# Two chained transformer blocks on one core: token blocks of the split activations 132 columns apart, and rows of scales, queries, attention visits and norm inputs moved

## The chip, the cores and the metric

The kernel runs on one core of a Trainium2 chip (trn2). The metric is the device time of one execution in microseconds (us).

## The reference

256 tokens of width 1024 go through two blocks of two layers each. Every layer is a mixer and a feed-forward part, each behind a norm and added to the stream x. The mixers are, in order: attention with forget gates (fox), attention with a compressed key and value (MLA), gated linear attention in chunks of 64 tokens (GLA), and a short convolution. Cut to what matters:

```
for layer in range(2):                                   # first block
    h = rms_norm(x, norm_mix_g[layer])
    x = x + (fox_mixer(h, ...) if layer == 0 else mla_mixer(h, ...))
    x = x + sq_relu_mlp(rms_norm(x, norm_ffn_g[layer]), w_up, w_down)
x = rms_norm(x, final_norm_g)
for i in range(2):                                       # second block
    h = rmsnorm(x, norm_mix_g_2[i])
    x = x + (gla_mixer(h, ...) if i == 0 else short_conv_mixer(h, ...))
    x = x + conv_ffn(rmsnorm(x, norm_ffn_g_2[i]), w_up, conv_w, w_down)
return rmsnorm(x, final_norm_g_2)
```

In the fox mixer the logits are `q @ k * scale + cum(query) - cum(key)`, where `cum` is a running sum of log sigmoids; in GLA the keys and queries are multiplied by exponentials of such sums, and the scores of a chunk are masked.

## The kernel before

All weights come from memory in float32. Each matrix product is made of three: a value is split into a high part (a cast to the matmul's own 32-bit format) and a low part (what is left), and a product is `hh*wh + hh*wl + hl*wh`. ACT casts the weights (L294), DVE subtracts for their low part (L312). The activations' parts hh and hl lie in tiles of the class Act, [128, 4, 256]: 128 rows of the width, four such blocks k, 256 tokens (L92). The token halves t=0 and t=1 of one k lie 128 columns, 512 bytes, apart.

Three shapes of products fill most of the time. `proj_T` (L391) makes a transposed result: 128 weight columns are loaded as the stationary operand, and the 256 tokens of hh or hl move past. `proj` and `accum` make rows of tokens: 128 tokens of hh or hl are stationary, and 512 weight columns move. `proj_wide` (L421) does the same with 264 columns. All go through `mmw` (L341), which lets the moving operand run alternately through its two halves; the distance within a pair is 512 bytes in `proj_T`, 1024 in `proj` and `accum`, 528 in `proj_wide`.

The order of the work is set in two steps. The program calls `tick()` after each group of 3 matmuls of 512 columns or 6 of 256. A step that has to come later is put into a queue with `after(n, fn)` and is emitted n ticks later; the distances stand in the list DLY. The visits of the two attentions come from a generator that is asked every so many ticks, by the tables FOX and MLA: each entry has a number of ticks and the heads whose weighted sum, transposes and logits are then emitted. A tile scheduler then puts each engine's instructions into their order.

The places that the change touches:

- `make_row` (L137) copies two columns of per-token scales on DVE to full width (L144), transposes them on PE (L523) and copies the result on ACT into a row "rowb". Rows scale transposed results (`by_row`, L419).
- `norm` (L588): an x tile that a projection has finished is transposed DLY[1] ticks later (`prep`, L523) and multiplied by the gain on DVE (L546); DLY[0] ticks later it is split (`split`, L509 on ACT, L512 on DVE). In `final_norm` (L1106), at the end of the first block, every x tile is also multiplied by a gain row (L1122), and, once POOL has the statistics of all four, by a scale (L1136). This ends at the entry of GLA, whose first product is a `proj_wide`.
- `split_pair` (L1368) and `split_ctx` (L729) split hidden values (L1373 on ACT, L1374 on DVE) and attention results.
- `fox` (L820): log sigmoids and their running sums (`cumulate`, DLY[6]), then visits by FOX. `mla` (L993): visits by MLA. In a visit, probabilities p (L697, L707, L716) are transposed (L533), copied to pT (L725), and used for the weighted sum (`pT,v` on L339).
- `gla` (L1151): `proj_T` of keys into PSUM tiles named acc, `proj_T` of queries into tiles named up, both scaled from PSUM on DVE (L419) and multiplied into kT (L1232) and qT (L1240). Then `core` (L1261) makes masked scores in up tiles, while the next projections also use up tiles.

`mmw` in full:

```
def mmw(self, out, lhsT, rhs, start, stop):
    self.mm(out.rearrange("p (b a) -> p b a", a=2), lhsT, rhs.rearrange("p (a b) -> p b a", a=2), start, stop)
```

## Time and profile before

| | us |
|---|---|
| median of 3 runs | 1104.34 |
| the runs | 1104.15, 1104.34, 2274.76 |
| the profiled execution | 1104.49 |
| its span in the trace | 1102.7 |

The span runs from the first to the last instruction of the trace; the profiled execution's own time is 1.8 us more. TensorE's granted clock was 0.997 of full speed, the upper of its two levels, so times of matmuls can be compared between stages. In the trace, PE is a matmul, PEld a weight load, which overlaps the matmul before it; DVE, ACT and POOL are the vector, scalar and GpSimd engines. A form is a group of like instructions with their shapes. In the trace's names, hh, hl, wh and wl are the parts of activations and weights, up, acc and tp PSUM tiles, and "out<-in" lists the operands of an instruction; with matmuls the first of the two inputs is the one that moves.

### The profile page before, as it was taken

How to read it: one execution, taken by the hardware profiler on the slowest of the kernel's cores; microseconds unless marked ns; L12 is line 12 of the kernel's file. 1: busy time of each engine (PE TensorE's matmuls, PEld its weight loads, DVE VectorE, ACT ScalarE, POOL GpSimd, SP SyncE). 2: the span in 40 equal slices, each digit the busy share in tenths (PEclk: the TensorE clock that was granted, in tenths of full speed). 3: DMA queues.
4: the chain of work that ended last, by engine and by line, in shares of the span. 5: the costliest groups of instructions: out<-in, count | busy, mean ns of one | idle time of the engine just before them, and what ended most of it. 6: DMA issues, size and time to landing. Idle time of an engine off the chain costs nothing.

```text
span 1102.7 us, 19201 instructions
## 1 busy us (share of the span) xinstructions
PE 1087.3 (99%) x7769; PEld 1003.4 (91%) x7769; DVE 801.4 (73%) x1200; ACT 609.2 (55%) x927; POOL 30.4 (3%) x55
## 2 busy tenths in 40 slices
PE   9999999999999999999999999999999999999997
PEld 7987999999988999999897899999999999999996
DVE  6687756556687766555788578787787768987786
ACT  6466655445665555545664556555555446565563
POOL 1000000000000000000010000000000000000001
PEclk9999999999999999999999999999999999999998
DMA  9844466655563566665555354566665664657551
GB/s 335 298 165 145 162 195 206 210 193 173 142 207 128 172 192 204 206 200 192 194 180 183 108 178 155 179 197 217 201 220 193 197 204 153 189 194 224 188 166 74
DMA packets 137801, 207.30 MB, mean 188 GB/s; under 512 B 10528, under 2 KB 65008, under 8 KB 137712
## 3 DMA queue, kind: packets, MB, share of 16 engines
q1 hardware_dynamic: 136576, 203.89, 56.8%
q10 hardware_dynamic: 1136, 2.17, 0.5%
q8 instruction: 61, 1.00, 0.4%
q14 instruction: 28, 0.23, 0.1%
HBM read 204.97 MB, written 1.07 MB: 187 GB/s over the span
## 4 chain that ended last, share of the span: by engine, by line
PE 87%; DVE 7%; ACT 2%; DMA 1%; issue 1%; SPq 0%; ACTq 0%; DVEq 0%
PE up L339 52%; PE acc L339 33%; DVE wl L312 2%; DMA raw<-fox_w_in 1%; ACT wh L294 1%; PE acc L523 1%; PE tp L523 1%; ACT p L697 1%; DVE p L716 1%; DVE x L602 0%; DVE p L707 0%; PE tp L533 0%; DVE tmp L1365 0%; DVE pT L725 0%; DVE kT L1232 0%
## 5 line engine op out<-in xcount | busy, mean ns | idle before, releaser
L312 DVE TENSOR_TENSOR wl<-raw,wh 128x1024 fp32r<-128x1024 f32 (+2 forms) x373 | 452.3, 1219 | 223.4 <-ACT wh L294 222.4
L294 ACT CAST wh<-raw 128x1024 fp32r<-128x1024 f32 (+2 forms) x373 | 388.8, 1043 | 381.7 <-PE up L339 253.1
L339 PE MATMUL up<-hh,wh 128*128 128x256 f32 x1564 | 431.7, 276 | 0.0
L339 PE MATMUL up<-hh,wl 128*128 128x256 f32 x1564 | 430.1, 275 | 0.0
L339 PE MATMUL up<-hl,wh 128*128 128x256 f32 x1564 | 429.4, 275 | 0.0
L339 PEld LDWEIGHTS up<-hh,wh 128*128 128x128 f32 x1564 | 300.1, 192 | 2.9 <-issue 1.5
L339 PEld LDWEIGHTS up<-hh,wl 128*128 128x128 f32 x1564 | 300.1, 192 | 0.9
L339 PEld LDWEIGHTS up<-hl,wh 128*128 128x128 f32 x1564 | 299.8, 192 | 0.3 <-DVE hl L512 0.2
L339 PE MATMUL acc<-wh,hh 128*128 128x512 f32 (+1 forms) x606 | 227.4, 375 | 0.2 <-DVE mx L716 0.2
L339 PE MATMUL acc<-wh,hl 128*128 128x512 f32 (+1 forms) x606 | 225.1, 371 | 0.1
L339 PE MATMUL acc<-wl,hh 128*128 128x512 f32 (+1 forms) x606 | 224.8, 371 | 0.0
L339 PEld LDWEIGHTS acc<-wh,hl 128*128 128x128 f32 x606 | 114.5, 189 | 15.4 <-DVE hl L1374 0.5
L339 PEld LDWEIGHTS acc<-wh,hh 128*128 128x128 f32 x606 | 114.6, 189 | 15.0 <-DVE mx L716 0.6
L339 PEld LDWEIGHTS acc<-wl,hh 128*128 128x128 f32 x606 | 114.7, 189 | 13.4
L1365 DVE SCALAR_TENSOR_TENSOR tmp<-tmp,vecs,tmp 128x255 f32<-128x255 f32 x192 | 78.0, 479 | 15.2 <-ACT tmp L1363 15.2
L339 PE MATMUL up<-wh,hh 128*128 128x512 f32 (+4 forms) x142 | 52.2, 370 | 1.8 <-DVE tmp L419 1.8
L339 PE MATMUL up<-wl,hh 128*128 128x512 f32 (+4 forms) x142 | 49.9, 352 | 0.2 <-DVE wl L312 0.2
L339 PE MATMUL up<-wh,hl 128*128 128x512 f32 (+4 forms) x142 | 49.8, 353 | 0.1
L1363 ACT ACTIVATE tmp<-tmp,vecs 128x256 f32<-128x256 f32 x96 | 40.9, 496 | 0.0
L1373 ACT CAST hh<-tmp 128x512 fp32r<-128x512 f32 x58 | 34.1, 619 | 8.3 <-DVE tmp L1418 8.3
L1374 DVE TENSOR_TENSOR hl<-tmp,hh 128x512 fp32r<-128x512 f32 x58 | 38.3, 685 | 0.0
L339 PEld LDWEIGHTS up<-wh,hh 128*128 128x128 f32 x142 | 26.8, 189 | 8.1 <-issue 5.5
(205 smaller groups left out, 769.8 us busy)
## 6 DMA issues: line engine op xcount, KB each, us to landing
raw<-ffn_w_up SPq DMA_DIRECT2D x176, 256.0 KB, 4.2
raw<-ffn_w_up SPq DMA_DIRECT2D x32, 1024.0 KB, 5.3
raw<-ffn_w_down SPq DMA_DIRECT2D x32, 1024.0 KB, 5.0
raw<-ffn_w_down SPq DMA_DIRECT2D x44, 512.0 KB, 6.6
raw<-sc_w_in SPq DMA_DIRECT2D x12, 1024.0 KB, 5.3
raw<-fox_w_in SPq DMA_DIRECT2D x10, 1024.0 KB, 9.7
raw<-gla_w_in SPq DMA_DIRECT2D x10, 1024.0 KB, 5.0
raw<-fox_w_out SPq DMA_DIRECT2D x4, 1024.0 KB, 5.2
```

Of the source, the lines that this page charges most:

```text
L294: self.last_hi = nc.scalar.copy(hi[:, :kn, :w], self.raws[r][:, k:k + kn])
L312: self.last_wl = nc.vector.tensor_tensor(out=u.lo[:, :kn, :w], in0=self.raws[r][:, k:k + kn], in1=u.hi[:, :kn, :w].bitcast(F32), op=ALU.su ...
L339: self.nc.tensor.matmul(out, lhsT, rhs, start=start, stop=stop, skip_group_check=True)
L523: self.nc.tensor.transpose(tp[:, i * P:(i + 1) * P], src[:, i * P:(i + 1) * P], self.ident)
L697: self.nc.scalar.activation(out=p[:, o:o + n], in_=p[:, o:o + n], func=AF.Exp, scale=scale, bias=nm[:, j:j + 1], accum_out=sm[:, j:j + 1])
L716: self.nc.vector.tensor_tensor_reduce(out=p[:, o:o + n], in0=lgs[h][:, w], in1=bias(h)[:, w], scale=1.0, scalar=NEG, op0=ALU.add, op1=ALU. ...
L1363: nc.scalar.activation(out=out, in_=z, func=AF.Copy, scale=w[:, 2:3])
L1365: nc.vector.scalar_tensor_tensor(out=out[:, d:], in0=z[:, :S - d], scalar=w[:, 2 - d:3 - d], in1=out[:, d:], op0=ALU.mult, op1=ALU.add)
L1373: nc.scalar.copy(hi, src)
L1374: nc.vector.tensor_tensor(out=lo, in0=src, in1=hi.bitcast(F32), op=ALU.subtract)
```

## The change

Six edits are made together.

1. The tiles of hh and hl become [128, 4, 2, 132], of which 128 columns are used: the two token halves lie 528 bytes apart. `block`, `get`, `split_ctx`, `split_pair` and `mmw` follow.
2. `make_row` emits the copy on DVE at once, and the transposes and the ACT copy three ticks later.
3. `setup_consts`, which converts a mask to integers, is called by `gla` in place of `fox`, and writes over a constant that is no longer used; the gate's weight tile becomes 384 columns wide.
4. GLA's queries are projected into acc tiles.
5. FOX and MLA get other numbers: the visits of the first come at ticks 6, 12, 18, 24, 30, 36, 42, 47, 54, 59, 64 and 66 of its stage (before: 8, 14, 20, 26, 32, 38, 43, 47, 52, 57, 62, 64), and the last but two of the second one tick earlier, the last at its old one.
6. DLY[0] is 4 (5), DLY[1] is 5 (4), DLY[6] is 8 (6): x tiles are transposed a tick later and split a tick sooner after that; the running sums come two ticks later.

```diff
--- before.py
+++ after.py
@@ -25,6 +25,8 @@
 MLA_H = 8
 GLA_H = 4
 WIDE = 512 + 16
+
+TOK = P + 4
 
 
 VEC = {}
@@ -89,15 +91,15 @@
     def group(self, g):
 
         if g not in self.tiles:
-            new = lambda tag: self.kb.h_p.tile([P, 4, S], F32R, tag=tag, name=self.kb.name(tag))
+            new = lambda tag: self.kb.h_p.tile([P, 4, 2, TOK], F32R, tag=tag, name=self.kb.name(tag))[:, :, :, :P]
             self.tiles[g] = new("hh"), new("hl")
         return self.tiles[g]
 
     def block(self, k, n, t=None):
 
-        sl = slice(0, S) if t is None else slice(t * P, (t + 1) * P)
         assert k % 4 + n <= 4
-        return [x[:, k % 4:k % 4 + n, sl] for x in self.group(k // 4)]
+        xs = [x[:, k % 4:k % 4 + n] for x in self.group(k // 4)]
+        return xs if t is None else [x[:, :, t] for x in xs]
 
     def put(self, k, n, t=None):
         self.ok.update((tt, k + i) for tt in (range(2) if t is None else [t]) for i in range(n))
@@ -108,7 +110,7 @@
 
     def get(self, t, k):
         self.wait(t, k)
-        return [x[:, k % 4, t * P:(t + 1) * P] for x in self.tiles[k // 4]]
+        return [x[:, k % 4, t] for x in self.tiles[k // 4]]
 
     def both(self, k):
 
@@ -121,7 +123,7 @@
 
 
     def __init__(self, kb, tile):
-        self.kb, self.tile, self.ok, self.rows = kb, tile, set(), {}
+        self.kb, self.tile, self.ok, self.rows, self.asked = kb, tile, set(), {}, set()
 
     def set(self, *cols):
         self.ok.update(cols)
@@ -134,24 +136,29 @@
         self.wait(i[1].start, i[1].stop)
         return self.tile[i]
 
-    def make_row(self, c, tp=None):
-
-        if c in self.rows:
+    def make_row(self, c, tp=None, gap=3):
+
+        if c in self.asked:
             return
+        self.asked.add(c)
         kb, nc = self.kb, self.kb.nc
         self.wait(c, c + 2)
         wide = kb.tmp_tile()
         nc.vector.tensor_copy(wide[:, :S].rearrange("p (t n) -> p t n", t=2),
                               self.tile[:, c:c + 2].unsqueeze(2).to_broadcast([P, 2, P]))
-        tp = kb.transpose4(wide, 2, tp if tp is None else lambda: tp)
-        row = kb.small.tile([P, S], F32, tag="rowb", name=kb.name("rowb"), bufs=2)
-        nc.scalar.copy(row, tp[:, :S])
-        self.rows[c] = row
+
+        def turn():
+            bank = kb.transpose4(wide, 2, None if tp is None else lambda: tp)
+            row = kb.small.tile([P, S], F32, tag="rowb", name=kb.name("rowb"), bufs=2)
+            nc.scalar.copy(row, bank[:, :S])
+            self.rows[c] = row
+
+        kb.after(gap, turn)
 
     def row(self, c, n=2):
 
         while c not in self.rows:
-            if c in self.ok and c + 1 in self.ok:
+            if c in self.ok and c + 1 in self.ok and c not in self.asked:
                 self.make_row(c)
             else:
                 self.kb.force()
@@ -341,7 +348,8 @@
     def mmw(self, out, lhsT, rhs, start, stop):
 
 
-        self.mm(out.rearrange("p (b a) -> p b a", a=2), lhsT, rhs.rearrange("p (a b) -> p b a", a=2), start, stop)
+        rhs = rhs.rearrange("p (a b) -> p b a", a=2) if len(rhs.shape) == 2 else rhs.rearrange("p a b -> p b a")
+        self.mm(out.rearrange("p (b a) -> p b a", a=2), lhsT, rhs, start, stop)
 
     @staticmethod
     def woven(ps, n=1):
@@ -728,6 +736,7 @@
 
     def split_ctx(self, cx, act, k):
         nc = self.nc
+        cx = cx.rearrange("p (t s) -> p t s", t=2)
         hi, lo = [x[:, 0] for x in act.block(k, 1)]
         nc.scalar.copy(hi, cx)
         nc.vector.tensor_tensor(out=lo, in0=cx, in1=hi.bitcast(F32), op=ALU.subtract)
@@ -852,8 +861,6 @@
                                            scalar=rs[:, t:t + 1], in1=bf, op0=ALU.mult, op1=ALU.add)
 
         self.proj_wide(h, evvf, self.acc_tile)
-        with self.tc.issue_after(self.last_wl.ins):
-            self.setup_consts()
         self.log_sigmoid(z, z, e, 32)
         ctok = self.att.tile([P, 2, 16], F32, tag="ctok", name="ctok")
         cneg = self.att.tile([16, 384], F32, tag="cneg", name="cneg")
@@ -1152,7 +1159,8 @@
         nc = self.nc
         a = self.a
         H = GLA_H
-        wg = self.att.tile([P, 512], F32, tag="cneg", name="wg")
+        self.setup_consts()
+        wg = self.att.tile([P, 384], F32, tag="cneg", name="wg")
         with self.tc.issue_after(self.last_hi.ins):
 
             for hd in range(H):
@@ -1344,7 +1352,7 @@
             self.after(DLY[21], lambda: self.prep(yy, t, list(range(4 * j, 4 * j + 4)), [(y, None)]))
 
         self.proj_T(h, 8, ev_k, self.acc_tile)
-        self.proj_T(h, 8, ev_q)
+        self.proj_T(h, 8, ev_q, self.acc_tile)
         while self.q:
             self.force()
         self.side = core()
@@ -1368,7 +1376,7 @@
     def split_pair(self, src, act, k0):
 
         nc = self.nc
-        src = src.rearrange("p (i s) -> p i s", i=2)
+        src = src.rearrange("p (i t s) -> p i t s", i=2, t=2)
         hi, lo = act.block(k0, 2)
         nc.scalar.copy(hi, src)
         nc.vector.tensor_tensor(out=lo, in0=src, in1=hi.bitcast(F32), op=ALU.subtract)
@@ -1564,7 +1572,8 @@
 
     def setup_consts(self):
         nc = self.nc
-        self.gmask_i = self.const.tile([P, P], I32, name="gmask_i")
+
+        self.gmask_i = self.cst("triu").bitcast(I32)
         nc.vector.tensor_copy(self.gmask_i, self.cst("gmask"))
 
     def start(self, h, stat):
@@ -1682,14 +1691,14 @@
 
 
 
-FOX = [(8, [], [], [0]), (6, [], [], [1]), (6, [], [0], [2]), (6, [0], [1], [3]), (6, [1], [2], [4]), (6, [2], [3], [5]),
...
+FOX = [(6, [], [], [0]), (6, [], [], [1]), (6, [], [0], [2]), (6, [0], [1], [3]), (6, [1], [2], [4]), (6, [2], [3], [5]),
...
-       (7, [], [2], []), (4, [2], [3], []), (2, [3], [], [])]
+       (6, [], [2], []), (4, [2], [3], []), (3, [3], [], [])]
...
-DLY = [5, 4, 11, 2, 2, 3, 6, 4, 6, 2, 11, 4, 6, 2, 6, 8, 5, 1, 1, 2, 2, 5, 1, 3, 2, 1, 3, 4, 8, 2, 2, 2, 1, 1, 1, 1]
+DLY = [4, 5, 11, 2, 2, 3, 8, 4, 6, 2, 11, 4, 6, 2, 6, 8, 5, 1, 1, 2, 2, 5, 1, 3, 2, 1, 3, 4, 8, 2, 2, 2, 1, 1, 1, 1]
```

The line numbers of the changed kernel are 3 to 8 higher at the same code.

**DVE at the entry of GLA.** Before, from the last multiplication by the norm's gain (tmp from tp, g) on; hl_5863 is the low part of the blocks k = 4 to 7, x_100 to x_103 are the stream's tiles, row_4081 is a gain row and rs_4084 POOL's statistics:

```order
L512 TENSOR_TENSOR hl_5749<-tmp_5719,hh_5748 128x4x128
L546 TENSOR_TENSOR tmp_5808<-tp_5803,g_4079 128x512
L312 TENSOR_TENSOR wl_5777<-raw_5626,wh_5776 128x2x512
L1122 TENSOR_TENSOR x_101<-x_101,row_4081 128x512
L512 TENSOR_TENSOR hl_5863<-tmp_5794,hh_5862 128x4x128
L312 TENSOR_TENSOR wl_5825<-raw_5626,wh_5824 128x2x512
L512 TENSOR_TENSOR hl_5863<-tmp_5808,hh_5862 128x4x128
L1122 TENSOR_TENSOR x_103<-x_103,row_4081 128x512
L1136 TENSOR_SCALAR x_100<-x_100,rs_4084 128x512
L1136 TENSOR_SCALAR x_102<-x_102,rs_4084 128x512
L1136 TENSOR_SCALAR x_101<-x_101,rs_4084 128x512
L312 TENSOR_TENSOR wl_5880<-raw_5660,wh_5879 128x2x512
```

In the change the same place reads (hl_5862 is the low part of k = 4 to 7, row_4079 and rs_4082 are the row and the statistics):

```order
L554 TENSOR_TENSOR tmp_5800<-tp_5795,g_4077 128x512
L319 TENSOR_TENSOR wl_5776<-raw_5624,wh_5775 128x2x512
L554 TENSOR_TENSOR tmp_5813<-tp_5808,g_4077 128x512
L1129 TENSOR_TENSOR x_101<-x_101,row_4079 128x512
L520 TENSOR_TENSOR hl_5862<-tmp_5800,hh_5861 128x4x128
L319 TENSOR_TENSOR wl_5824<-raw_5624,wh_5823 128x2x512
L1129 TENSOR_TENSOR x_103<-x_103,row_4079 128x512
L1143 TENSOR_SCALAR x_100<-x_100,rs_4082 128x512
L1143 TENSOR_SCALAR x_102<-x_102,rs_4082 128x512
L1143 TENSOR_SCALAR x_101<-x_101,rs_4082 128x512
L520 TENSOR_TENSOR hl_5862<-tmp_5813,hh_5861 128x4x128
L319 TENSOR_TENSOR wl_5879<-raw_5658,wh_5878 128x2x512
```

The second split of hl (k = 4 to 7) stood ahead of the gain row's last multiplication and of the three scalings by rs; now it stands behind them. Of the splits of k = 0 to 3 (low part hl_5749 before, hl_5747 in the change) the first stood 7 rows ahead of the first row shown of before; in the change both stand behind the addition into x_103:

```order
L612 SCALAR_TENSOR_TENSOR x_101<-acc_4377,rs_3140,x_101 128x512
L1129 TENSOR_TENSOR x_102<-x_102,row_4079 128x512
L612 SCALAR_TENSOR_TENSOR x_103<-acc_4378,rs_3140,x_103 128x512
L520 TENSOR_TENSOR hl_5747<-tmp_5710,hh_5746 128x4x128
L520 TENSOR_TENSOR hl_5747<-tmp_5720,hh_5746 128x4x128
```

The first split moved behind three instructions on x.

**DVE at GLA's queries.** Before, up_6212 and up_6213 are the PSUM tiles of the queries, rowb_5964 is the row of scales:

```order
L312 TENSOR_TENSOR wl_6273<-raw_6092,wh_6272 128x2x512
L312 TENSOR_TENSOR wl_6303<-raw_6092,wh_6302 128x2x512
L419 SCALAR_TENSOR_TENSOR tmp_6324<-up_6212,rowb_5964 128x256 x2
L419 SCALAR_TENSOR_TENSOR tmp_6334<-up_6213,rowb_5964 128x256
L1240 TENSOR_TENSOR qT_5765<-tmp_6324,qT_5765 128x512
L419 SCALAR_TENSOR_TENSOR tmp_6334<-up_6213,rowb_5964 128x256
L312 TENSOR_TENSOR wl_6341<-raw_6150,wh_6340 128x2x512
L1240 TENSOR_TENSOR qT_5765<-tmp_6334,qT_5765 128x512
```

In the change:

```order
L319 TENSOR_TENSOR wl_6272<-raw_6091,wh_6271 128x2x512
L319 TENSOR_TENSOR wl_6302<-raw_6091,wh_6301 128x2x512
L427 SCALAR_TENSOR_TENSOR tmp_6323<-acc_6211,rowb_5972 128x256 x2
L427 SCALAR_TENSOR_TENSOR tmp_6333<-acc_6212,rowb_5972 128x256
L1248 TENSOR_TENSOR qT_5764<-tmp_6323,qT_5764 128x512
L427 SCALAR_TENSOR_TENSOR tmp_6333<-acc_6212,rowb_5972 128x256
L319 TENSOR_TENSOR wl_6340<-raw_6149,wh_6339 128x2x512
L1248 TENSOR_TENSOR qT_5764<-tmp_6333,qT_5764 128x512
```

The order of DVE is the same; the four scalings read acc tiles in place of up tiles.

**PE at a row of scales of MLA.** Before, tmp_3474 is the copy of the scales, and tp_3518 a transposed norm input:

```order
L339 MATMUL acc_3439<-hh_3319,wh_3354 128x256
L339 MATMUL acc_3439<-hh_3319,wl_3355 128x256
L339 MATMUL acc_3439<-hl_3320,wh_3354 128x256
L523 MATMUL tp_3518<-ident,tmp_3422 128x128
L523 MATMUL acc_3473<-ident,tmp_3474 128x128 x2
L523 MATMUL tp_3518<-ident,tmp_3422 128x128 x3
```

In the change, the transposes of the copy (tmp_3473) stand 27 rows behind those of the norm input (tp_3512):

```order
L346 MATMUL up_3523<-hh_3431,wh_3376 128x256
L346 MATMUL up_3523<-hh_3431,wl_3377 128x256
L346 MATMUL up_3523<-hl_3432,wh_3376 128x256
L346 MATMUL up_3523<-hh_3431,wh_3376 128x256
L346 MATMUL up_3523<-hh_3431,wl_3377 128x256
L531 MATMUL acc_3472<-ident,tmp_3473 128x128 x2
```

The two transposes went from the midst of the norm input's transposes to a place among the matmuls of 256 columns.

## Rows read from the trace of the kernel before

**Rows 1.** Page, its head, list of engines and chain by engine:

```profile
span 1102.7 us, 19201 instructions
...
PE 1087.3 (99%) x7769; PEld 1003.4 (91%) x7769; DVE 801.4 (73%) x1200; ACT 609.2 (55%) x927; POOL 30.4 (3%) x55
...
PE 87%; DVE 7%; ACT 2%; DMA 1%; issue 1%; SPq 0%; ACTq 0%; DVEq 0%
```

**Rows 2.** Groups by form, whole span: busy us, mean ns | idle before:

```profile
L339 PE MATMUL up<-hh,wh 128*128 128x256 f32 x1564 | 431.7, 276 | 0.0
...
L339 PE MATMUL acc<-wh,hh 128*128 128x512 f32 x558 | 214.0, 384 | 0.2 <-DVE mx L716 0.2
...
L339 PE MATMUL acc<-wh,hh 128*128 128x264 f32 x48 | 13.3, 278 | 0.0
```

**Rows 3.** Chain in order of time: start us, us, what:

```profile
24.77 7.88 PE acc L339 x70
...
152.98 10.72 PE up L339 x96
163.69 10.36 PE acc L339 x48
```

**Rows 4.** Timeline of PE at 38 us: start us, us, engine, line, what:

```profile
38.25 0.81 PE L339 MATMUL acc<-z,csts 128*128 128x16 f32 x6 [0.25 <-issue]
```

**Rows 5.** Groups by form of PE, from 38.2 to 38.9 us:

```profile
L339 PE MATMUL acc<-z,csts 128*128 128x16 f32 x6 | 0.8, 261 | 0.2 <-issue 0.2
```

**Rows 6.** Groups by form, whole span, the splits' second halves on DVE:

```profile
L1374 DVE TENSOR_TENSOR hl<-tmp,hh 128x512 fp32r<-128x512 f32 x58 | 38.3, 685 | 0.0
...
L512 DVE TENSOR_TENSOR hl<-tmp,hh 128x512 fp32r<-128x512 f32 x24 | 16.0, 686 | 0.5
```

**Rows 7.** Waits of PE and PEld: us in total, times, longest us:

```profile
PE up L339 <- DVE tmp L419: 1.8, 1, 1.8
...
PE tp L533 <- DVE pT L725: 0.6, 1, 0.6
PE up L339 <- DVE pT L725: 0.5, 1, 0.5
PE tp L523 <- DVE tmp L144: 0.4, 1, 0.4
PE acc L523 <- DVE tmp L144: 0.4, 1, 0.4
PE tp L533 <- DVE p L707: 0.3, 1, 0.3
...
PE acc L339 <- DVE mx L716: 0.2, 1, 0.2
...
PEld acc L523 <- DVE x L602: 1.1, 4, 0.3
```

**Rows 8.** Timeline of DVE from 543 to 557 us:

```profile
546.51 0.68 DVE L546 TENSOR_TENSOR tmp<-tp,g 128x512 f32<-128x512 f32 x1
...
552.02 0.68 DVE L512 TENSOR_TENSOR hl<-tmp,hh 128x512 fp32r<-128x512 f32 x1
...
554.17 1.31 DVE L1136 TENSOR_SCALAR x<-x,rs 128x512 f32<-128x512 f32 x3 [0.86 <-POOL rs L563]
```

**Rows 9.** Timeline of PE from 544 to 557 us:

```profile
544.67 0.28 PE L339 MATMUL up<-wh,hh 128*128 128x264 f32 x1
...
552.34 0.28 PE L339 MATMUL up<-wh,hh 128*128 128x264 f32 x1
552.76 0.38 PE L339 MATMUL up<-wh,hl 128*128 128x264 f32 x1
```

**Rows 10.** Windows: us, busy of PE, PEld, DVE, ACT, POOL; clock, DMA:

```profile
568.00:580.00 12.00, 12.00 (x106) 11.87 (x105) 11.97 (x19) 7.88 (x12) 0.00 (x0) 1.00 0.46 143
580.00:594.00 14.00, 12.25 (x103) 11.74 (x102) 14.00 (x22) 7.87 (x9) 0.00 (x0) 1.00 0.52 183
```

**Rows 11.** Timeline of DVE from 589.5 to 596 us:

```profile
595.09 0.69 DVE L1240 TENSOR_TENSOR qT<-tmp,qT 128x512 f32<-128x512 f32 x1
```

More of the change, by code (lines that the diff above doesn't have):

```diff
@@ L1679, in body @@
         self.flush()
-FOX = [(8, [], [], [0]), (6, [], [], [1]), (6, [], [0], [2]), (6, [0], [1], [3]), (6, [1], [2], [4]), (6, [2], [3], [5]),
-       (5, [3], [4], [6]), (4, [], [5], [7]), (5, [4], [6], []), (5, [5], [7], []), (5, [6], [], []), (2, [7], [], [])]
+FOX = [(6, [], [], [0]), (6, [], [], [1]), (6, [], [0], [2]), (6, [0], [1], [3]), (6, [1], [2], [4]), (6, [2], [3], [5]),
+       (6, [3], [4], [6]), (5, [], [5], [7]), (7, [4], [6], []), (5, [5], [7], []), (5, [6], [], []), (2, [7], [], [])]
 MLA = [(0, [], [], [0]), (4, [], [], [1]), (7, [], [0], []), (5, [0], [1], []), (3, [1], [], [2]), (4, [], [], [3]),
-       (7, [], [2], []), (4, [2], [3], []), (2, [3], [], [])]
+       (6, [], [2], []), (4, [2], [3], []), (3, [3], [], [])]
 WARM = (10, 3)
-DLY = [5, 4, 11, 2, 2, 3, 6, 4, 6, 2, 11, 4, 6, 2, 6, 8, 5, 1, 1, 2, 2, 5, 1, 3, 2, 1, 3, 4, 8, 2, 2, 2, 1, 1, 1, 1]
+DLY = [4, 5, 11, 2, 2, 3, 8, 4, 6, 2, 11, 4, 6, 2, 6, 8, 5, 1, 1, 2, 2, 5, 1, 3, 2, 1, 3, 4, 8, 2, 2, 2, 1, 1, 1, 1]
 @with_exitstack
```

## Prediction

> **What bounds the kernel now.** I read the page first: its list of engines, then its chain. TensorE is busy 1087.3 of 1102.7 us in 7769 matmuls, and the chain that ended last is 87% PE and 7% DVE [rows 1]. So there are two ways to gain: a shorter distance between matmuls, or less of the some 15 us in which PE stands still. An edit on DVE or ACT counts only where PE waits for it.
>
> The groups by form come next. The long one is the 256-column matmul of the transposed projections: three forms of 1564 each (one is shown), 4692 matmuls. The 512-column ones that make rows of tokens are 558 of each of three forms, the 264-column ones 48 of each [rows 2]. A form's mean (276, 384, 278 ns) is the length of one and not the distance to the next, as matmuls overlap. The distance comes from the chain in order of time, where PE runs unbroken: 7.88 us / 70 = 112.6 ns at 264 columns, 10.72 / 96 = 111.7 ns at 256, 10.36 / 48 = 215.8 ns at 512 [rows 3].
>
> Last come PE's waits, which are few and short: 1.8 us once for a scaled query, 0.6 and 0.5 for transposed probabilities, 0.4 twice for the copy from which a row of scales is transposed, 0.3 and 0.2 for probabilities and a maximum [rows 7]. All the moved work of this change is about these, some 4 us in total.
>
> **The change part by part.** The sum is made against the profiled execution, 1104.49 us (the span and 1.8 us around it); the median of the runs is 1104.34, 0.15 lower.
>
> *Token blocks 132 columns apart.* In a 256-column matmul the moving operand alternates between two blocks of 128 tokens; their distance goes from 512 to 528 bytes. What could that give? From 264 to 512 columns the distance grows by (215.8 - 112.6) / 248 = 0.416 ns a column, so 256 columns would be 112.6 - 8 x 0.416 = 109.2 ns. The trace has 111.7 [rows 3]. If the 512-byte distance costs these 2.4 to 2.5 ns, the edit gives 4692 x 2.44 = 11.4 us. Two rows speak against it. The 512-column matmuls alternate too, at 1024 bytes, and lie on the same line as the 264-column ones, at 528 bytes. And six matmuls of only 16 columns, each with a weight load of 128 columns, take 0.81 us, of which the last is 0.26: (0.81 - 0.26) / 5 = 0.110 us apart [rows 4, 5]. Sixteen columns cannot need that; the weight load does. So a load of 128 columns sets a floor of about 0.11 us, and 256-column matmuls stand on it whatever their operand's step. Gain: 0, bounds -11.4 and 0.
>
> The Trainium skill ("TensorE: Matmul & The Clock Gate", section Back-to-back issue gap) gives 262 cycles for 256 columns, and says that in a stream of loads and matmuls both set the spacing. The first half would leave the 2.4 ns to be explained by the step, the second by the load; rows 3 to 5 bear out the second. The Trainium skill's page "SBUF — State Buffer" (in the note on cachelines under Door 1: The DMA port swizzle) says that each access that crosses to a new 16-byte line pays; alternating blocks cross at every element at either distance, so by it the edit gives nothing, and rows 3 show no such price at all.
>
> The splits that write the tiles now write 128-column pieces in both forms. The cost is known: the form already cut by token block takes 686 ns on DVE, the contiguous one 685 [rows 6]. Where the tile is a stationary operand, its 128 columns stay contiguous and only their start moves by 16 bytes. No row shows such a start: nearest are the loads from 528-column weight tiles, which run at 111.7 ns like the others. I take 0; a load twice as long is the other end and a rival below.
>
> *Constants and the gate tile.* The mask conversion is one short DVE instruction that moves into the first stage, the gate tile shrinks: 0, bounds -0.2 and +0.4 (one short wait like those of rows 7).
>
> *Rows of scales.* Copy and transposes were one step; now three ticks (nine matmuls of 512 columns, or eighteen of 256, some 2 us) lie between. That covers the two waits of 0.4 us [rows 7]. The transposes stay as many; the scalar copy behind them comes later, and its first reader, the scaling of queries or keys, is asked for ticks later. Gain 0.8, bounds -0.8 and +0.5 (the reader then waits as long as the longest wait for a transposed tile, rows 7).
>
> *Attention visits.* The first attention starts its visits two ticks earlier and spreads them; the second gets three more 512-column matmuls (0.65 us) in front of its last weighted sum, more than the 0.5 us waited there. In the first, 0.6 + 0.3 + 0.2 us are waited [rows 7]. DVE has no room there, since weight residues and probabilities share it, so I take 1.0 of these 1.1 us with their refill, and 0.5 for the second: -1.5, bounds -2.2 and +0.5.
>
> *Norm inputs.* Transposes of x stand one tick later, their splits one earlier: weight loads wait 4 times 0.3 us for x at such stage ends [rows 7], most of it under running matmuls. I take -0.4, bounds -1.1 and +0.5.
>
> *Entry of gated linear attention.* Here the new order costs something. The split of the first token block stood in front of two later results of x on DVE; now it stands behind them, ending some 0.7 us after 546.51, where the four additions end [rows 8]. PE ends the down projection at 544.67 [rows 9] and has eight 264-column matmuls (0.9 us) and one set of transposes before the first use, so it comes at about 546.0 and waits 1.1 us. The last split is worse: before, it ran at 552.02, and PE waited 0.3 us for it (the gap before 552.76 in rows 9). Now it stands behind three scalings that wait 0.86 us for POOL's statistics and end at 555.4 [rows 8], so it ends near 556.1. PE would be there at 546.0 + 1.1 + 65 x 0.1126 + 0.3 = 554.7. The two waits are 1.1 + 1.4, less the 0.3 that goes: +2.2 on PE.
>
> Not all of it lasts. From 568 to 594 us DVE is busy 25.97 of 26.00 us [rows 10], and PE stands 1.8 us at its end for a scaled query [rows 7]. DVE's own work is not more than before, so a PE that comes 2.2 us late eats that slack. What lasts is 2.2 - 1.8 = 0.4 us, if DVE keeps its time; bounds 0 and +2.9.
>
> *Queries of gated linear attention in the acc tiles.* The 1.8 us went to free the two up tiles that the queries held. The next matmuls into up tiles no longer wait. But DVE's order is the same; the masked scores need the scaled queries, whose last product starts at 595.09 [rows 11], so PE runs into the same DVE a few matmuls later. I take -0.2; bounds -1.8 and +0.5.
>
> Sum: 0 + 0 - 0.8 - 1.5 - 0.4 + 0.4 - 0.2 = -2.5. 1104.49 - 2.5 = 1102.0 as a profiled execution, 1101.8 as a median; I say 1102.
>
> **The rivals.**
> 1. *The step does set the distance.* For: 256 columns are the only form off the line, by 2.4 ns, and the only one at 512 bytes. Against: rows 4 and 5. Price: -11.4 on top, 1102 - 11.4 = 1090.6.
> 2. *The entry's waits last (slower).* Place: DVE's queue at 546 to 556 us, the splits behind additions and scalings. For: the order, and POOL's chain that nothing shortens. It decides if DVE falls behind with PE (its weight residues need casts that wait for PE to free buffers), so that the 1.8 us of slack is not there, and if the visits and rows only move their waits. Price: +2.9, with -0.5 left of the other terms: 1104.34 + 2.4 = 1106.7.
> 3. *Every wait comes back.* DVE is the engine that the attention waits for, and its work doesn't shrink; what PE no longer waits at one visit it waits at the next. For: 7% of the chain is DVE. Against: the added matmuls stand right at the waits. Price: 0, 1104.3.
> 4. *Shifted starts slow the loads.* Stationary blocks of the second token half start at odd multiples of 16 bytes. If their loads took twice 0.11 us, each of 558 x 3 / 2 = 837 512-column matmuls would be at least 0.22 - 0.2158 = 0.004 us longer and each of 48 x 3 / 2 = 72 264-column ones 0.11: 3 + 8 = +11, so 1102 + 11 = 1113. Nothing in the rows speaks for it beyond that none excludes it.
> 5. *Both halves of gated linear attention go well:* no entry wait, the 1.8 us kept: 1102 - 2 = 1100.
>
> **How the numbers follow.** Forecast 1102 (from 1100.8 to 1103.6): 0.45. Rival 1: 0.12. Rival 2: 0.15. Rival 3: 0.13. Rival 4: 0.03. Rival 5: 0.12. The range leaves out rival 4 and the far tails of 1 and 2: from 1090 to 1107; the forecast's own is 1100.8 to 1103.6. A change of 2% (22 us), about what a measurement of this kernel can tell from no change, lies outside every case, also rival 1 with all other bounds on its side (-11.4 - 6). What is left for mechanisms that I haven't seen: 0.02 faster, 0.02 slower, 0.96 within.
>
> **What would show it.** Right: 256-column matmuls still 111.7 ns apart in unbroken pieces of the chain; PE without the 0.4-us waits for the copied scales; the wait for a scaled query of 1.8 us gone or below 0.5; new PE waits for hl at the entry of gated linear attention, 1 us each. Wrong: 109.2 ns there (rival 1, the sum falls by 11); 264-column matmuls at more than 112.6 ns (rival 4); new waits of half a microsecond at the attention visits or at rows of scales (rival 3); DVE ending the scaled queries more than 1 us later than PE's lag explains (rival 2).

## The result, and the profile after

The changed kernel took 1110.88 us (median of 5 runs, 1109.83 to 1112.41), the one before 1104.31 on the same chip: ratio 1.0062, 95% interval 1.0051 to 1.0074. It is 6.6 us slower; 1102 was predicted, and the range ended at 1107.

The page of the profile after, to be held against [rows 1]:

```profile
span 1109.1 us, 19206 instructions
...
PE 1089.1 (98%) x7769; PEld 1004.9 (91%) x7769; DVE 801.5 (72%) x1200; ACT 609.2 (55%) x927; POOL 29.3 (3%) x55
...
PE 85%; DVE 8%; ACT 2%; DMA 2%; issue 1%; SPq 1%; POOL 0%; ACTq 0%; DVEq 0%
```

The span is 6.4 us longer (1109.1 for 1102.7) with the same 7769 matmuls. PE stands still 4.6 us more and is busy 1.8 us more; most of these 1.8 us are matmuls that ran at a lower clock, as told below. The share of PE on the chain falls from 87 to 85%. The chain in order of time shows that the long stretches did not change; the 96 matmuls of 256 columns and the 48 of 512 [rows 3] still take 10.72 and 10.36 us, now some 4.8 us later:

```profile
157.75 10.72 PE up L346 x96
168.47 10.36 PE acc L346 x48
```

PE's waits (us in total, times, longest) answer to [rows 7]:

```profile
PE up L346 <- DVE hl L520: 2.5, 3, 1.4
PE up L346 <- DVE qT L1248: 1.6, 2, 0.9
...
PE acc L346 <- DVE kT L424: 1.3, 1, 1.3
PE up L346 <- ACT v L624: 1.3, 1, 1.3
PE tp L531 <- ACT tmp L624: 1.2, 1, 1.2
PE up L346 <- DVE rc L712: 0.7, 1, 0.7
```

None of the waits of [rows 7] for DVE's scaled query, copied scales, pT, p or mx is left; these have taken their place. In place of the 1.8 us for a scaled query, two of 0.7 and 0.9 us for the multiplied queries qT stand there.

Where the 6.4 us arise is read best by counting matmuls. Both traces have 7769; the n-th of one is held against the n-th of the other, and the table says by how much the lag grew from one row to the next, for the changed kernel and for the runs told below (starts in the trace of before: matmul 400 at 58.1 us, 900 at 125.1, 2900 at 416.9, 3700 at 539.0, 4000 at 580.9, 4400 at 650.9, 7700 at 1080.7). Each row is one profiled execution, which need not lie at its kernel's median (e1's took 1107.94, e5's 1106.77, e7's 1112.46).

```
                          to 400  first    to     to     GLA    GLA      rest   in
                                  attent.  2900   3700   entry  queries         all
after                     +0.27   +4.51   -0.41   0.00  +1.81   -0.22  +0.45   +6.40
e1 FOX old                +0.28   +0.18   -0.41   0.00  +1.82   +1.38  +0.21   +3.46
e2 last logits at 47      +0.02   +1.29   -0.41   0.00  +1.81   -0.22  +0.20   +2.70
e3 fifth visit at 32      -0.35   +4.69   -0.40   0.00  +1.82   +1.39  +0.46   +7.61
e4 layout only            -0.45   -0.09   -0.01   0.00   0.00   -0.03  -0.01   -0.58
e5 norm delays old        -0.01   +2.79   -0.53   0.00  +0.29   -0.22  -0.03   +2.30
e6 queries in up           0.00   +2.90   -0.40   0.00  +1.82    0.00  +0.45   +4.76
e7 rows at once           +0.11   +6.46   -0.26   0.00  +1.68   -0.24  +0.21   +7.97
e8 before, new FOX        -0.26   +4.45   -0.03   0.00  -0.01   -0.01  -0.27   +3.87
f1 FOX and norm old       -0.23    0.00   -0.53   0.00  +0.70   -0.21  -0.29   -0.57
f2 as f1, early visits    +0.29   +0.96   -0.53   0.00  +0.69   -0.21  -0.29   +0.91
f3 as f1, late room       +0.19   -0.09   -0.53   0.00  +0.70   +1.39  -0.29   +1.36
f4 FOX old, split sooner  +0.17   -0.09   -0.53   0.00  +1.38   -0.21  -0.29   +0.43
g1 before, last at 48     -0.21   +5.11   -0.02   0.00   0.00   -0.01  -0.27   +4.61
g2 second attention only  -0.85   +0.21   -0.39   0.00   0.00   -0.01  -0.01   -1.05
```

So there are two places: the first attention (+4.5) and the entry of gated linear attention (+1.8). Everything else together is +0.1. The first column differs by up to 0.9 us between executions of like code (-0.21 in g1 and -0.85 in g2, which change nothing there), and the seventh comes in two levels some 0.25 apart (e8 and g1 against e4) whose origin was not looked for; the clock adds to the second and sixth, as told below.

In the first attention the timeline of PE (start us, us) shows two waits of 1.3 us. The first, at the fifth visit:

```profile
74.89 0.22 PE L541 MATMUL acc<-ident,p 64*128 64x64 f32 x1
76.45 0.93 PE L346 MATMUL acc<-kT,qT 64*128 64x128 f32 x8 [1.34 <-DVE kT L424]
```

At 76.45 the logits of the fifth visit come straight behind the projection that makes their keys: DVE has still to scale them. The second wait, with the last matmul of the projection of v in front of it and the matmuls behind it:

```profile
92.00 0.38 PE L346 MATMUL up<-wh,hl 128*128 128x512 f32 x1
...
96.17 1.43 PE L346 MATMUL up<-kT,qT 64*128 64x128 f32 x4 [1.29 <-ACT v L624]
97.53 0.80 PE L346 MATMUL acc<-wh,hl 128*128 128x512 f32 x1
98.12 0.63 PE L346 MATMUL acc<-wh,hh 128*128 128x512 f32 x1
98.55 0.63 PE L346 MATMUL acc<-wl,hh 128*128 128x512 f32 x1
...
100.06 0.38 PE L346 MATMUL acc<-wh,hl 128*128 128x512 f32 x1
100.28 0.38 PE L346 MATMUL acc<-wh,hh 128*128 128x512 f32 x1
```

At 96.17 the second half of the last logits waits for a PSUM tile that ACT has not emptied (v). The tile was full at 92.4 us, where its last matmul ends (92.00 and 0.38). ACT's timeline has the copy behind four exponentials, which first wait 1.22 us for DVE:

```profile
93.68 0.40 ACT L705 ACTIVATE p<-p,nm 128x128 f32<-128x128 f32 x1 [1.22 <-DVE nm L804]
...
94.96 0.49 ACT L705 ACTIVATE p<-p,nm 128x256 f32<-128x256 f32 x1
...
95.45 0.67 ACT L624 ACTIVATE v<-up,rs 128x512 f32<-128x512 f32 x1
```

So ACT stood still while the tile was ready: by this timeline it is the order on ACT that makes PE wait, not the amount of ACT's work. No run tried another order.

Behind the wait the 512-column matmuls are 0.43 us apart (98.12 to 98.55), from 100.06 on again 0.22. The windows say why (us, busy time of PE, PEld, DVE, ACT, POOL, granted clock, DMA):

```profile
94.00:96.00 2.00, 0.89 (x4) 0.30 (x2) 0.53 (x4) 2.00 (x9) 0.00 (x0) 1.00 0.87 339
96.00:98.00 2.00, 1.83 (x5) 1.18 (x6) 1.45 (x10) 1.43 (x3) 0.00 (x0) 0.61 0.02 6
98.00:100.00 2.00, 2.00 (x6) 1.55 (x6) 1.83 (x6) 0.00 (x0) 1.13 (x2) 0.54 0.00 0
100.00:102.00 2.00, 2.00 (x11) 1.74 (x10) 0.45 (x1) 1.52 (x4) 0.00 (x0) 1.00 0.03 8
```

PE is busy 0.89 of 2.00 us while it waits, and in the next 4 us the granted clock is 0.61 and 0.54: part of the time at the lower of its two levels (1.2 for 2.4 GHz). That is where the matmuls stand 0.43 us apart.

At the entry of gated linear attention the timeline of PE has two waits for hl:

```profile
551.18 0.38 PE L346 MATMUL up<-wh,hl 128*128 128x264 f32 x1 [0.62 <-DVE hl L520]
...
560.53 0.38 PE L346 MATMUL up<-wh,hl 128*128 128x264 f32 x1 [1.41 <-DVE hl L520]
```

The timeline of DVE there:

```profile
550.44 1.28 DVE L520 TENSOR_TENSOR hl<-tmp,hh 128x512 fp32r<-128x512 f32 x2
...
558.57 1.30 DVE L1143 TENSOR_SCALAR x<-x,rs 128x512 f32<-128x512 f32 x3 [1.14 <-POOL rs L571]
559.80 0.68 DVE L520 TENSOR_TENSOR hl<-tmp,hh 128x512 fp32r<-128x512 f32 x1
```

These are the places of the prediction: the first splits (550.44) stand behind the additions, the last (559.80) behind the three scalings that wait for POOL (1.14 us; 0.86 before, [rows 8]). The waits are 0.62 and 1.41 us; 1.1 and 1.4 had been worked out.

### The profile page after: what moved, and what is told of

It reads as the page before. It is cut to its first block, busy times and chain, and to the rows that moved or that the text cites. A ratio compares the mean times of both kernels' runs of the same rounds, so it can differ in the third digit from the quotient of the medians.

```text
span 1109.1 us, 19206 instructions
## 1 busy us (share of the span) xinstructions
PE 1089.1 (98%) x7769; PEld 1004.9 (91%) x7769; DVE 801.5 (72%) x1200; ACT 609.2 (55%) x927; POOL 29.3 (3%) x55
## 4 chain that ended last, share of the span: by engine, by line
PE 85%; DVE 8%; ACT 2%; DMA 2%; issue 1%; SPq 1%; POOL 0%; ACTq 0%; DVEq 0%
PE up L346 49%; PE acc L346 33%; DVE wl L319 3%; PE acc L531 1%; DMA bias<-rows 1%; DMA raw<-fox_w_in 1%; ACT p L705 1%; ACT wh L301 1%; DVE p L724 1%; PE tp L531 1%; DVE p L715 0%; DVE hl L520 0%; DVE x L610 0%; SPq L271 0%; DVE tmp L1373 0%
## 5 line engine op out<-in xcount | busy, mean ns | idle before, releaser
L346 PE MATMUL up<-hh,wh 128*128 128x256 f32 x1532 | 423.1, 276 | 0.7 <-DVE rc L712 0.7
L346 PE MATMUL up<-hl,wh 128*128 128x256 f32 x1532 | 420.9, 276 | 0.5 <-DVE hl L520 0.5
L346 PE MATMUL up<-hh,wl 128*128 128x256 f32 x1532 | 420.8, 275 | 0.0
L346 PEld LDWEIGHTS up<-hh,wh 128*128 128x128 f32 x1532 | 294.0, 192 | 4.3 <-issue 2.4
L346 PEld LDWEIGHTS up<-hh,wl 128*128 128x128 f32 x1532 | 294.0, 192 | 0.9
L346 PEld LDWEIGHTS up<-hl,wh 128*128 128x128 f32 x1532 | 293.7, 192 | 1.1 <-DVE hl L520 0.9
L1382 DVE TENSOR_TENSOR hl<-tmp,hh 128x512 fp32r<-128x512 f32 x58 | 38.2, 684 | 0.0
```

The lines of the kernel that those rows point to most:

```text
L346: self.nc.tensor.matmul(out, lhsT, rhs, start=start, stop=stop, skip_group_check=True)
L1382: nc.vector.tensor_tensor(out=lo, in0=src, in1=hi.bitcast(F32), op=ALU.subtract)
```

## Experiments

All ratios are against runs of the kernel before on the same chip. The theory after the result was: the new visits of the first attention cost 4.9 us, the norm inputs' delays some 2, and nothing else counts.

**e1: the changed kernel with FOX of before.**

```diff
-FOX = [(6, [], [], [0]), (6, [], [], [1]), (6, [], [0], [2]), (6, [0], [1], [3]), (6, [1], [2], [4]), (6, [2], [3], [5]),
...
+FOX = [(8, [], [], [0]), (6, [], [], [1]), (6, [], [0], [2]), (6, [0], [1], [3]), (6, [1], [2], [4]), (6, [2], [3], [5]),
...
```

> The changed kernel with the FOX table of before; all else as in the change. Theory (the new visits cost the time): by the traces PE is 4.8 us behind before at the end of the first attention; this goes, so 1110.9 - 4.8 = 1106.1, and the waits on kT (1.3), on ACT's v (1.3) and the half clock at 96 to 100 us are not there. Rival (the running sums, two ticks later, or the rows of scales make the first attention late): the visits then wait for the same data elsewhere, and the time stays at 1109 to 1111.

Measured: 1105.99, ratio 1.0018 (1.0009 to 1.0027). The lag of the first attention falls from +4.51 to +0.18, and both waits are gone. As the theory had it. (The trace's +3.46 in all holds +1.38 from a lower clock at the queries of gated linear attention, told at the end.)

**e8: the other way round, the kernel before with the new FOX.**

> The kernel before with the changed FOX table, nothing else. Theory (the table alone makes the loss of the first attention): 1104.3 + 4.9 = 1109.2, with waits on kT and on ACT's v and a half clock behind the second. Rival (it needs the later running sums or rows beside it): 1104 to 1106.

Measured: 1108.54, ratio 1.0040 (1.0028 to 1.0053); the same waits on kT (1.3) and on v (1.3), and the lag of the first attention +4.45. The table alone makes the loss; neither the later sums nor the rows of scales are needed for it.

**e2: one number apart from the change: the last logits a tick sooner.** Why should that matter? The table's sums are not the ticks at which the visits come. A visit waits for its keys to be finished; with the new table the fifth would come at tick 30, the keys are there at 31, and all later visits move along: 31, 37, 43, 48, 55 in place of 30, 36, 42, 47, 54 (the list in the section on the change gives the sums, not the ticks). At tick 48 the projection of v has been emitted, and from there on the visits take their PSUM tiles from the pool "up" (`late` is set), which that projection still holds.

```diff
-       (6, [3], [4], [6]), (5, [], [5], [7]), (7, [4], [6], []), (5, [5], [7], []), (5, [6], [], []), (2, [7], [], [])]
+       (6, [3], [4], [6]), (4, [], [5], [7]), (8, [4], [6], []), (5, [5], [7], []), (5, [6], [], []), (2, [7], [], [])]
```

> The changed kernel with one number of FOX moved: the visit with the last logits comes one tick sooner after the one before it (4 for 5), the next one a tick later after that (8 for 7), so that only this visit moves, from tick 48 to 47. Theory: at 47 the last logits still go to acc tiles, the wait of 1.3 us for ACT's v is gone and with it the half clock behind it: about -1.4 - 1.6 = -3.0, 1107.9. Rival (DVE is simply behind at this place and PE waits for it at any visit): a wait of the same length at tick 47, 1110 to 1111.

Measured: 1107.14, ratio 1.0028 (1.0017 to 1.0039), 3.7 us less than the change. The wait for ACT is gone; left in the first attention are those on kT and, at 59 us, on DVE's nm (0.7 for rc in the change):

```profile
PE acc L346 <- DVE kT L424: 1.3, 1, 1.3
...
PE up L346 <- DVE nm L804: 1.1, 1, 1.1
```

The windows around the moved visit:

```profile
92.00:97.00 5.00, 4.80 (x36) 3.47 (x35) 4.50 (x27) 3.78 (x12) 0.99 (x2) 1.00 0.64 210
97.00:102.00 5.00, 5.00 (x37) 3.89 (x37) 3.85 (x8) 4.83 (x13) 0.00 (x0) 1.00 0.02 3
```

With PE busy 4.80 of 5.00 us the granted clock stays 1.00. So the rival (a wait of the same length wherever the visit is) falls.

**g1: the kernel before with the same visit one tick later,** nothing else: one number up, the next one down, so that the last logits come at 48 and all others stay.

```diff
-       (5, [3], [4], [6]), (4, [], [5], [7]), (5, [4], [6], []), (5, [5], [7], []), (5, [6], [], []), (2, [7], [], [])]
+       (5, [3], [4], [6]), (5, [], [5], [7]), (4, [4], [6], []), (5, [5], [7], []), (5, [6], [], []), (2, [7], [], [])]
```

> The kernel before with one visit of FOX one tick later: the last logits at tick 48 in place of 47, all others where they were. Theory (the last logits' place is the larger part of the loss: behind tick 47 they go to up tiles, wait for ACT to empty one, and the halved clock follows): 1104.3 + 2 to 3 = 1106.3 to 1107.3, with the wait for ACT's v. Rival (it costs only together with the earlier visits' backlog): 1104.0 to 1105.0.

Measured: 1108.81, ratio 1.0036 (1.0024 to 1.0049), 4.5 us for one tick, more than expected: the wait for ACT is 2.1 us here, and the lower clock lasts longer. Its row of the waits:

```profile
PE up L339 <- ACT v L616: 2.1, 1, 2.1
```

And its windows:

```profile
92.00:94.00 2.00, 0.87 (x4) 0.30 (x2) 0.80 (x4) 1.51 (x7) 0.00 (x0) 1.00 1.00 345
94.00:96.00 2.00, 1.02 (x4) 0.92 (x4) 1.48 (x8) 2.00 (x5) 0.00 (x0) 0.68 0.28 108
96.00:98.00 2.00, 2.00 (x6) 1.18 (x5) 1.34 (x7) 0.23 (x1) 0.64 (x2) 0.50 0.00 0
98.00:100.00 2.00, 2.00 (x6) 1.64 (x5) 0.85 (x2) 0.06 (x1) 0.50 (x2) 0.50 0.03 8
100.00:102.00 2.00, 2.00 (x11) 0.95 (x10) 0.98 (x1) 2.00 (x6) 0.00 (x0) 0.61 0.00 0
```

This settles the larger part of the loss: it is the last logits' place behind tick 47, and it needs no backlog from earlier visits. That the tile is what counts there is read from the wait; a run with the last logits at 48 in acc tiles was not made.

**e3: the fifth visit at tick 32, as before, in the changed kernel.**

```diff
-(6, [1], [2], [4]), (6, [2], [3], [5]),
+(8, [1], [2], [4]), (5, [2], [3], [5]),
```

> The changed kernel with the logits of head pair 4 at tick 32 (as in before) in place of 31, where the check for finished keys had put them; all other visits stay on their ticks. Theory: one tick between the scaling of the keys and the logits takes most of the 1.3 us wait on kT: -1.0 to -1.5, 1109.4 to 1109.9, the wait of the last logits stays. Rival (the wait is DVE's backlog from the earlier visits): the wait is the same or moves, 1110.5 to 1111.

Measured: 1112.13, ratio 1.0073 (1.0060 to 1.0087), no gain, and above the ranges of theory and rival. The wait on kT falls from 1.3 to 0.7 us, but the one for ACT's v grows from 1.3 to 1.9. In kind the rival was right: what PE no longer waits at the fifth visit, it waits at the last.

**f1, f2, f3: FOX and the norm delays of before, and then single parts of the new visits.** f1 keeps the layout, rows, queries, second attention and sums of the change; f2 is f1 with the first four visits two ticks earlier; f3 is f1 with the visits behind the last logits two ticks later.

> The changed kernel with FOX and the norm inputs' two delays of before: what is left are the layout, the rows of scales, the queries in acc tiles, the second attention's visits, the later sums. Theory: each of the two losses goes by its own amount, 1110.9 - 4.9 - 2.3 = 1103.7, a little under before (the second attention gains 0.3 to 0.5, the queries 0.2, the rows 0.2). Rival (the losses cover one another, the waits at the scaled queries remain and halve the clock there): 1105 to 1106.

> As f1, with the first four visits of FOX two ticks earlier, as in the change, and the fifth and all later ones on the ticks of before (32, 38, 43, 47, ...). Theory (it is the fifth visit's place, beside the keys' scaling, and the last logits' tile that cost): the early visits by themselves take the wait of 0.5 us at 61 us away, 1103.2. Rival (DVE's backlog from early visits costs, as the run with the fifth visit at 32 suggested): 1104.5 to 1106.

> As f1, with the visits behind the last logits two ticks later (54, 59, 64, 66 in place of 52, 57, 62, 64), as the change has them but for its delay. Theory: the last waits are in front of tick 52, so nothing is gained there: 1103.7 within 0.5. Rival (the room is what the transposes need): 1103 or less.

Measured: f1 1104.33 (1.0005, 0.9996 to 1.0014), f2 1105.05 (1.0009, 1.0001 to 1.0018), f3 1104.09 (1.0003, 0.9994 to 1.0011). f1 takes the whole loss back and gains nothing. Early visits by themselves cost some tenths, where the theory had a gain: f2 is 0.7 us over f1, which the intervals do not separate, but its trace shows the lag of the first attention at +0.96, with waits of 0.7 on kT and 0.8 on nm. So the wait on kT is not the fifth visit's place alone; 0.7 of the 1.3 us stays when it comes at 32, in f2 as in e3. The later visits change nothing that can be measured.

**e5 and f4: the norm inputs.** e5 is the change with DLY[0] and DLY[1] of before (5, 4); f4 has FOX of before and 4, 4: transposes where they were, splits a tick sooner.

> The changed kernel with the norm inputs' two delays of before (transposes after 4 ticks, splits after 5); all else as in the change. Theory: the waits for hl at the entry of gated linear attention (two, 0.5 to 1.4 us) go with the old order of DVE, PE is 1.8 us less behind there, and the 0.16 us at three later stage ends go: 1110.9 - 2.3 = 1108.6. Rival (the slack that the prediction named: PE then comes earlier to the scaled queries and waits there for the same DVE): 1110.4 to 1110.9.

> The changed kernel with FOX of before and with the norm inputs transposed after 4 ticks, as in before, but split after 4 in place of 5. Theory (the later transposes push the splits behind additions and scalings at the entry of gated linear attention): with the transposes back the waits for hl go and the time is that of f1 or some tenths less. Rival (the sooner split is what reorders DVE): 1105.5 to 1106, as with both delays of the change.

Measured: e5 1107.97 (1.0032, 1.0021 to 1.0044), 2.9 less than the change; f4 1105.12 (1.0010, 1.0002 to 1.0019). In e5 the lag at the entry falls from +1.81 to +0.29 and that of later stage ends from +0.45 to -0.03. How much of the 2.9 us is the clock can't be told: e5's profiled execution shows no lower clock in the first attention (lag +2.79 there), but it took 1.2 us less than the median of e5's runs. Cleaner is e1 against f1, 1105.99 to 1104.33, -1.7, though the intervals of the two still overlap. f4 goes between the theories: with the transposes back PE still waits 1.6 us for one split, and the entry's lag is +1.38, against +0.70 in f1 and +1.82 in e1. So at the entry the sooner split makes more than the later transposes, against what I had expected. Over the whole kernel the two steps are alike by the medians (1104.33 to 1105.12 to 1105.99, neither clear of the intervals by itself), as the lag of later stage ends comes with the later transposes alone (-0.29 in f4 as in f1, +0.21 in e1). What the +0.70 of f1 is was not tried apart; its trace shows a wait of 0.55 us for ACT's v at 557.63.

**e4: layout and constants alone in the kernel before.**

```diff
-            new = lambda tag: self.kb.h_p.tile([P, 4, S], F32R, tag=tag, name=self.kb.name(tag))
+            new = lambda tag: self.kb.h_p.tile([P, 4, 2, TOK], F32R, tag=tag, name=self.kb.name(tag))[:, :, :, :P]
...
-            self.setup_consts()
...
+        self.setup_consts()
+        wg = self.att.tile([P, 384], F32, tag="cneg", name="wg")
```

> The kernel before with the token blocks 132 columns apart and the constants' edits that make room for it (mask conversion in the third mixer, narrower gate tile), nothing else. Theory (weight loads set the distance of 256-column matmuls): 1104.3 within 0.5, 111.7 ns apart as before. Rival 1 of the prediction: 109.2 ns apart, 1092.9. Rival 4: 264-column matmuls further apart than 112.6 ns, up to 1115.

Measured: 1104.29 against 1104.33, ratio 0.9998 (0.9989 to 1.0007). The chain has the same length for 96 matmuls of 256 columns at 528 bytes as at 512 [rows 3], and for 70 of 264 columns:

```profile
24.32 7.88 PE acc L341 x70
...
152.44 10.72 PE up L341 x96
```

**e6 and e7: queries in up tiles, rows of scales at once, in the changed kernel.**

```diff
-        self.proj_T(h, 8, ev_q, self.acc_tile)
+        self.proj_T(h, 8, ev_q)
```

> The changed kernel with the queries of gated linear attention in up tiles as in before. Theory: DVE's queue ends at the same time, so PE waits for the freed up tile in place of the masked scores: the wait on qT (1.6 in two) turns into one on the scaled queries, the time stays within 0.7 of 1110.9. Rival (the acc tiles are what costs, as the scores wait behind matmuls of other tiles): 1109.5 or less. Other rival (they save a wait): 1112 or more.

```diff
-        kb.after(gap, turn)
+        turn()
```

> The changed kernel with the rows of scales transposed and copied at once, as in before. Theory: the later transposes saved 0.8 us in the second mixer and cost 0.3 in the first, where PE now waits 1.2 us for ACT's scaled queries without them: 1110.9 + 0.5 = 1111.4. Rival (the late row is what DVE's scaling of the keys waits for in the first attention): the wait on kT goes, 1109.

Measured: e6 1109.83 (1.0051, 1.0039 to 1.0064), e7 1110.60 (1.0053, 1.0039 to 1.0066); the change has 1110.88. Neither is where its theory had it (within 0.7 of the change, and 1111.4), but both lie inside the spread that the lower clock makes, so the table's columns tell more. In e6 the queries' column goes from -0.22 to 0.00, and the old wait is back (1.7 us for tmp): the acc tiles gain 0.2 us. In e7 the columns of the start and of the second attention change by -0.16 and +0.15: the later rows gain nothing. The rival of e7 falls: the wait on kT is 1.3 us there too. The two executions also measure the clock: up to the end of the first attention e6, e7 and the change have the same visits, and their lags there are +2.90, +6.46 and +4.51, with this window for e6:

```profile
97.00:102.00 5.00, 5.00 (x29) 3.90 (x30) 3.83 (x12) 3.59 (x11) 1.13 (x2) 1.00 0.02 4
```

and this for e7:

```profile
97.00:102.00 5.00, 5.00 (x12) 3.53 (x12) 2.39 (x10) 1.41 (x3) 1.13 (x2) 0.50 0.01 3
```

**g2: the second attention's visits alone, in the kernel before.**

```diff
-       (7, [], [2], []), (4, [2], [3], []), (2, [3], [], [])]
+       (6, [], [2], []), (4, [2], [3], []), (3, [3], [], [])]
```

> The kernel before with the second attention's visits of the change, nothing else. Theory: three more 512-column matmuls in front of the weighted sum cover the 0.5 us that PE waited there for the transposed probabilities, and nothing comes in its place: 1104.3 - 0.4 = 1103.9. Rival (the wait moves to the last weighted sum): 1104.3.

Measured: 1103.94 against 1104.32, ratio 0.9997 (0.9988 to 1.0006): not to be told from no change by its time, but the trace shows the lag of the second attention at -0.39 and the wait of 0.5 us gone. With the 0.2 us of the queries in the trace it is the only part that gains, and the best of all versions by a margin that is inside its interval.

## Why the prediction was wrong

**The step that failed is the attention visits**, put at -1.5 with bounds -2.2 and +0.5. Its half for the second attention holds: -0.5 was forecast, -0.4 came. Its half for the first ("I take 1.0 of these 1.1 us", a gain) came out as +4.5. The prediction read the new ticks off the table and asked only whether each old wait had more work in front of it. It did not follow the check that holds a visit back until its keys are done. That check moves the fifth visit to the very tick of the keys' projection (a new wait of 1.3 us on kT, of which 0.7 stays in f2, where the fifth visit is at 32 and only the earlier ones have moved) and the last logits over the switch from acc to up tiles (1.3 us for ACT, which has the exponentials first). g1 shows the second to cost 4.5 us by itself, the lower clock included, e2 that taking it back gives 3.7. Neither place was among the rivals; rival 3, "every wait comes back", saw the kind but ended at no loss.

**A term that was missing is the clock.** The rows stood at a granted clock of 1.00 around all waits, and the prediction counted a wait at its length. In the profile after, waiting 1.3 us cost another 1.6: the lag of +4.51 against +2.90 of e6, which has the same visits.

**The layout (0)** is right: 256-column matmuls are 10.72 / 96 = 111.7 ns apart at either step, so the step does not set the distance. That the weight load sets it rests on rows 4 and 5; no run tried it. Rival 1 (-11.4) and rival 4 (+11) both fall with e4. **The constants (0)** are right with it.

**The entry of gated linear attention** was seen, and of its two waits the second was sized to the tenth, the first too long (1.1 + 1.4 forecast, 0.62 + 1.41 measured, lag +1.81 for +2.2). Wrong is what followed: 1.8 us of it were to vanish in DVE's slack, so that 0.4 would last. But DVE lags as much as PE. Its last multiplication of the queries in the profile after:

```profile
601.28 0.68 DVE L1248 TENSOR_TENSOR qT<-tmp,qT 128x512 f32<-128x512 f32 x1
```

That is 6.2 us later than before [rows 11], just PE's lag there, where at the three scalings (558.57 for 554.17 in [rows 8]) it was 4.4. This is the condition that rival 2 named, though not its sign (DVE later than PE's lag explains). The timelines show where DVE fell behind. Between the two places it waits 1.7 us in three for ACT's casts of weights (1.0 in two before), and a product of PE for the gate, for which it waited nothing before, holds it up by 0.93 us:

```profile
569.70 0.88 DVE L1208 TENSOR_SCALAR tmp<-acc,vecs 128x256 f32<-128x256 f32 x2 [0.93 <-PE acc L1203]
```

From 573.88 us on, up to the queries, each of DVE's instructions is 6.2 us later. The prediction took DVE's busy stretch from 568 us on as work that keeps its time, but that work starts from a result of PE. So 1.6 us last. **The queries** came as forecast (-0.2) wherever the clock stayed at 1.00 there.

**Norm inputs** (-0.4) went the other way: +0.45 over the later stage ends (-0.03 in e5), and 1.1 of the entry's lag (+1.82 in e1, +0.70 in f1); put back they give 1.7 us (e1 to f1). **Rows of scales** (-0.8) are 0 in effect: the two waits of 0.4 us are gone, but at the first PE now waits 1.2 us for ACT's scaled queries, which came behind the transposes before, and in the second mixer 0.5 us for a split (at 321.87). A wait's length in the table of waits is not the gain of removing it; what is late next behind it has to be read too.

In sum: forecast -0.8 -1.5 -0.4 +0.4 -0.2 = -2.5; measured on the trace 0 (rows), +4.5 and -0.4 (visits), about +0.5 (norm inputs at later stage ends), +1.8 -0.2 (gated linear attention), +0.27 at the start, 6.4 together.

## What to carry to other kernels

When an order is written as a table of distances, work out where each step really lands, with every condition that can hold it back and every switch (of a pool, of a phase) that lies between: one tick over such a switch cost 4.5 us here, and no single wait of the old profile was that long. Where the engine that feeds the critical one has little room (before, DVE is busy 10.99, 9.62 and 10.98 us of the three 12-us windows from 58 to 94 us, in this attention), moving a visit earlier moves the wait to the next visit; ask what is late next before a removed wait is counted as a gain. Look at the order on the engine that has to free a tile, and not only at its load: ACT stood still with the full tile waiting. And price a new stop of TensorE at more than its length.

## What the runs showed of the hardware

A stop of PE can bring the clock down after it. After a stretch of 2 us with PE busy 0.87 or 0.89 us the granted clock fell to 0.50 to 0.68 in the windows of the next 4 us (the change) and 8 us (g1), and 512-column matmuls ran 0.43 us apart in place of 0.22. It does not fall each time: e6 makes the same visits as the change, has the same wait of 1.29 us for v, and its clock stayed 1.00:

```profile
94.00:96.00 2.00, 0.71 (x4) 0.31 (x3) 0.61 (x5) 2.00 (x8) 0.00 (x0) 1.00 0.76 295
96.00:98.00 2.00, 2.00 (x10) 1.53 (x11) 1.96 (x13) 1.20 (x2) 0.40 (x1) 1.00 0.00 0
```

In the profile of the change the wait of 1.34 us at the fifth visit left the clock at 1.00, too (72 to 80 us). At the queries of gated linear attention the two waits of 0.7 and 0.9 us left the clock at 1.00 in the profile of the change, and in that of e1 brought it to 0.84 and 0.87:

```profile
594.00:600.00 6.00, 4.37 (x30) 3.14 (x29) 5.40 (x10) 1.28 (x2) 0.00 (x0) 0.84 0.63 236
600.00:606.00 6.00, 6.00 (x44) 4.04 (x44) 2.34 (x4) 1.98 (x3) 0.00 (x0) 0.87 0.51 175
```

So a kernel with such a stop has a wider spread: the change's runs lie within 1109.83 to 1112.41, 2.6 us, those of before in the largest set (33) within 1103.66 to 1105.10. The two waits at the queries have their price, too. Of the 55 executions of e1 and f1 to f4, which all have them, 15 stand apart from the rest by 0.9 to 1.3 us; two of these were profiled, e1's and f3's, and both show the lower clock there (+1.38 and +1.39 in the column of the queries, for -0.2). The kernel before has one wait of 1.8 us there, and its 33 show no such group. If all 15 have it there, which only the two profiles show, the price is 15/55 of these 1.6 us, an estimate of 0.4 us on average, against the 0.2 us that the acc tiles gain in an execution that stays at 1.00.
